# Weight halves interleaved word by word, and the merge's streams moved to 256-byte boundaries, in a float32 attention block on one core

## The chip, the core and the metric

The kernel runs on one core of a Trainium2 chip. The metric is device time in microseconds (us); lower is better. Three runs of the kernel before took 586.53 to 587.0 us, median 586.82. The profile below is of one further execution; its instructions span 584.6 us.

## What is computed

One hybrid decoder block on 512 tokens plus 16 learned meta tokens, model width 1,024, in float32. Cut to what matters here:

```python
u = rmsnorm(h, pre_norm_g[l])
proj = u @ w_in[l]
(cq, ckv, k_pe_raw, z_mla, fq, fk, fv, f_logit, z_fox, gate_a, gate_b) = jnp.split(proj, split_idx, axis=-1)
q = (rmsnorm(cq, ...) @ w_uq[l])            # 16 heads, 64 + 32 columns
kv = (rmsnorm(ckv, ...) @ w_ukv[l])
o_mla = causal_block_attention(q_m, k_m, v_mla, MLA_SCALE)
y_mla = (o_mla * jax.nn.silu(z_mla)) @ w_br_mla[l]
o_fox = causal_block_attention(fox_heads(fq), fox_heads(fk), fox_heads(fv), FOX_SCALE, cum)
y_fox = (o_fox * jax.nn.silu(z_fox)) @ w_br_fox[l]
mixed = (jax.nn.sigmoid(gate_a) * y_mla + jax.nn.sigmoid(gate_b) * y_fox) @ w_out[l]
h = h + rmsnorm(mixed, post_norm_g[l])
```

`proj` has 7,600 columns; 1,024 rows of weights stand behind each. Nearly all the work is products with weights.

## The kernel before, in words

**Precision by halves.** A float32 operand is split into an upper half (the value rounded to the engine's `float32r`) and a lower half (the rest). A product `w x a` becomes three matmuls into the same accumulator: upper weight with upper activation, upper weight with lower activation, lower weight with upper activation. `unit` (the work of one output tile) and `passes` issue them in that order for each of the eight 128-row blocks `k`.

**Who is stationary.** In a matmul `mm(out, x, y)` the operand `x` (128 x 128) is loaded into the array and `y` streams past it. For all projections (`fq`, `fk`, `v`, `z`, `pg`, `mq`, `mk`, `ppe`) and for the branch outputs (`py` and the merge's products `x`, `y`, `z`) the weight halves are stationary and the activations stream: 512 real tokens at once, or two streams of 272 and 256 tokens where the meta tokens are needed. In the last stage, the product with `w_out`, it is the other way: activations are stationary and 512 columns of weights stream.

**Where the operands lie.** `uTh` and `uTl` (the normed input, transposed, both halves) have rows of 576 words per block, so that the 512 real tokens of every block start at a multiple of 256 bytes. A weight passes through the pool `wp` with three buffers each of `wraw` (as it comes from memory), `wh` and `wl` (its halves), 128 x 1,024 words each; all start at a multiple of 256 bytes. In the built program `gh` and `gl` (halves of the gated attention output) start at 90,880 and 107,264 bytes, both 0 modulo 256; `a1h`, `a1l`, `a2h`, `a2l` (sums of it) at 161,216, 165,312, 169,408 and 177,600, and `tb0` to `tb3` (columns of `w_out`) from 128,448, all 192 modulo 256.

**How a weight is split.** `wload` issues the DMA into `wraw` on SP's queue. `wsplit` then has ScalarE (ACT) cast `raw` to `wh`, and POOL (later VectorE, DVE) compute `raw - wh` into `wl` in `split_lo`. `q_mla` does the same for two gathered pieces; `take` in `pair_py` splits sums of weights in halves of a room. Loads run up to three units ahead, splits about one to two units ahead.

**Order.** TensorE's order is written by hand (a list of steps for each attention stage: scores, then filling units, then values). The order on ACT and DVE comes from a scheduler that follows priorities and when operands and rooms become free. There are 16 attention stages of about 20 us; then the merge: four pairs of output tiles by products of 256 columns (seven products of 12 matmuls each per pair, three with streams from `a1`/`a2`, four from `gh`/`gl`), alternating with gate units `pg`; then `py`; then the product with `w_out`.

Every matmul and every weight load stands at line 98 of the profile (the helper `mm`), every subtraction at line 104, the casts at 131, 607 and 1119.

Of the kernel before, what the change touches and what calls it, by code (L numbers as in the profile page):

```python
# [11 lines left out]
F32 = mybir.dt.float32  # L12
F32R = mybir.dt.float32r
# [42 lines left out]
def block_kernel(ctx: ExitStack, tc: tile.TileContext, x, meta_tokens, pre_norm_g, w_in, fox_forget_b,  # L56
# [6 lines left out]
    wout = w_out[0].rearrange("(k p) f -> p k f", p=128)  # L63
# [20 lines left out]
    wp = ctx.enter_context(tc.tile_pool(name="wp", bufs=3))  # L84
    uid = [0]
# [3 lines left out]
    def dma(out, src, start=None):  # L89

        with tc.issue_after(sums_out[0]) if written[0] and sums_out else nullcontext():
            ins = (start or nc.sync.dma_start)(out=out, in_=src)
        if written[0]:
            tc.keep_in_program_order(ins)
        return ins.ins

    def mm(*a, **k):
        nc.tensor.matmul(*a, **k)  # L98
# [4 lines left out]
    def split_lo(eng, lo, src, hi):  # L103
        return eng.tensor_tensor(out=lo, in0=src, in1=f32(hi), op=ALU.subtract)  # L104

    def wload(srcs):

        uid[0] += 1
        u = uid[0]
        raw = wp.tile([128, 1024], F32, tag="wraw", name=f"wraw{u}")  # L110
        n = 0
        parts = []
        for src in srcs:
            dims = src.shape[1:]
            w = int(np.prod(dims))
            names = "abcd"[: len(dims)]
            pat = f"p ({' '.join(names)}) -> p {' '.join(names)}"
            rv = raw[:, n : n + w].rearrange(pat, **{c: d for c, d in zip(names, dims)})
            dma(rv, src)
            parts.append((n, w))  # L120
            n += w
        return u, raw, parts, n

    low = [nc.gpsimd]

    def wsplit(ld):

        u, raw, parts, n = ld
        wh, wl = (wp.tile([128, 1024], F32R, tag=t, name=f"{t}{u}") for t in ("wh", "wl"))
        with tc.issue_after(behind[0]) if behind else nullcontext():  # L130
            nc.scalar.copy(wh[:, :n], raw[:, :n])  # L131
        with tc.issue_after(held[0]) if held else nullcontext():
            split_lo(low[0], wl[:, :n], raw[:, :n], wh[:, :n])
        return [(wh[:, o : o + w], wl[:, o : o + w]) for o, w in parts]

    def wunit(srcs):
        return wsplit(wload(srcs))

    def weights(srcs, wrap):

# [12 lines left out]
    def by_k(part, nk):  # L153

        h, l = (t.rearrange("p (k f) -> p k f", k=nk) for t in part)
        return (lambda k: h[:, k, :]), (lambda k: l[:, k, :])
# [390 lines left out]
    with ExitStack() as att:  # L547
# [41 lines left out]
        def load_qp(pr):  # L589
            dma(f32(QP), qpe_dram[2 * pr : 2 * pr + 2].rearrange("h i x f s -> (h i x f) s"))  # L590

        def q_mla(pr):
            ld = []

            def load():
                if not ld:
                    ld.append(wload([wuq[:, :, 192 * pr : 192 * pr + 192], wukv[:, 256 * pr : 256 * pr + 256]]))

            def get():
                load()  # L600
                u, raw, _, _ = ld[0]
                wh, wl = (wp.tile([128, 1024], F32R, tag=t, name=f"{t}{u}") for t in ("wh", "wl"))
                cuts = [(raw[:, 0:384].rearrange("p (b e) -> p b e", e=96)[:, :, 0:NOPE], lambda t: t[:, 0:256].rearrange("p (b e) -> p b e", e=NOPE)),
                        (raw[:, 384:640].rearrange("p (h a e) -> p a h e", h=2, a=2), lambda t: t[:, 256:512].rearrange("p (a h e) -> p a h e", a=2, h=2))]
                for src, to in cuts:
                    with tc.issue_after(behind[0]) if behind else nullcontext():
                        nc.scalar.copy(to(wh), src)
                for src, to in cuts:
                    split_lo(nc.gpsimd, to(wl), src, to(wh))
                w = mw[pr] = [(wh[:, o : o + 128], wl[:, o : o + 128]) for o in range(0, 512, 128)]  # L610
                return (lambda k: w[k][0]), (lambda k: w[k][1])
            get.load = load

            halves = hl_done(("q", 0, pr), S, S)

            def q_done(i, ps):
                halves(i, ps)
                if pr:
                    load_qp(pr)
            return unit(f"mq{pr}", get, cq_act, 2, REAL, q_done)  # L620
# [441 lines left out]
    with ExitStack() as mg:  # L1062
        mg.enter_context(tc.manual_schedule(engines={mybir.EngineType.PE}))
        m1 = mg.enter_context(tc.tile_pool(name="m1", bufs=1, side="right"))
# [6 lines left out]
        tb = [m1.tile([128, HK, 512], F32, tag=f"tb{n}", name=f"tb{n}") for n in range(4)]  # L1071
        a1 = [m1.tile([128, HK, 256], F32R, tag=n, name=n) for n in ("a1h", "a1l")]
        a2 = [m1.tile([128, HK, S], F32R, tag=n, name=n) for n in ("a2h", "a2l")]
        mx = gT[0]
        sh, sl = ([t.rearrange("p k s -> p (k s)")[:, 1024 * j : 1024 * j + 1024].rearrange("p (k s) -> p k s", k=HK)
                   for j in range(4)] for t in uT0)
# [41 lines left out]
        def split_to(to, src):  # L1118
            nc.scalar.copy(to[0], src)  # L1119
            split_lo(nc.vector, to[1], src, to[0])  # L1120
# [6 lines left out]
        def comb(out, p, q, op=ALU.subtract):  # L1127
            nc.vector.tensor_tensor(out=out, in0=p, in1=q, op=op)  # L1128

        def pair_py(i, br):  # L1130

            j, g, wb = i + HK, gT[br], wbr[br]
            ra, rb = (wload([wb[:, :, 128 * f : 128 * f + 128]])[1] for f in (i, j))
            yield
            b11, b21, b12, b22 = ra[:, 0:512], ra[:, 512:], rb[:, 0:512], rb[:, 512:]
            X, Y, Z = (sp.tile([128, 512], F32, tag="s", name=f"{n}{i}{br}")[:, 0:256] for n in "xyz")
            c11, c21, c12, c22 = g[:, i, lo_], g[:, i, up], g[:, j, lo_], g[:, j, up]
            th1, th2 = ths[i, br], ths[j, br]
            room = []

            def take(src):
                if not room:
                    uid[0] += 1
                    hl = [wp.tile([128, 1024], F32R, tag=t, name=f"{t}{uid[0]}") for t in ("wh", "wl")]
                    room.extend([[t[:, sl] for t in hl] for sl in (slice(0, 512), slice(512, 1024))])
                to = room.pop(0)
                split_to(to, src)
                return to

            def prod(ps, a, w, first, last):  # L1150
                q = 0
                for k in range(HK):
                    for wx, ax in ((w[0], a[0]), (w[0], a[1]), (w[1], a[0])):
                        mm(ps, wx[:, 128 * k : 128 * k + 128], ax[:, k], start=(first and q == 0), stop=(last and q == 11),
                           skip_group_check=True)
                        q += 1

            def gated(dst, th, ts, ps, add):
                if add:
                    held[:] = [nc.vector.tensor_tensor(out=dst, in0=ps, in1=dst, op=ALU.add).ins]  # L1160
                return nc.vector.scalar_tensor_tensor(out=dst, in0=th[:, ts], scalar=1.0, in1=dst if add else ps, op0=ALU.add, op1=ALU.mult)

            w11 = take(b11)
            comb(b11, b12, b11)
            t1 = take(b11)
            yield
            comb(b12, b22, b12)
            comb(b11, b22, b11)
            t2 = take(b11)
            prod(X, A11, w11, True, False)  # L1170
            nc.scalar.copy(c11, X)
            w21 = take(b21)
            prod(Z, S1, t1, True, False)
            nc.scalar.copy(c22, Z)
            t3 = take(b12)
            comb(b21, b21, b11)
            prod(X, S2, t2, False, False)
            nc.scalar.copy(c12, X)
            w22 = take(b22)
            prod(Y, A12, w21, True, True)  # L1180
            gated(c11, th1, lo_, Y, True)
            t4 = take(b21)
            prod(X, S3, t3, False, False)
            gated(c22, th2, up, X, True)
            read = held[0]
            prod(Z, S4, w22, False, True)
            gated(c12, th2, lo_, Z, True)
            held[:] = [read]
            prod(X, A22, t4, False, True)
            closed[i] = gated(c21, th1, up, X, False).ins  # L1190
# [21 lines left out]
        for i in range(HK):  # L1212
# [5 lines left out]
            if i == 0:  # L1218
                for n, (q, c) in enumerate(((0, 0), (0, 1), (1, 1), (1, 0))):
                    for half in range(2):  # L1220
                        k0 = HK * q + 2 * half
# [30 lines left out]

        def plain(kb, n, c):
            k0 = HK * kb + 2 * c
            return by_k(wunit([wout[:, k0 : k0 + 2, 512 * n : 512 * n + 512]])[0], 2)

        def summed(n, c):
            uid[0] += 1
            raw = tb[n][:, 2 * c : 2 * c + 2].rearrange("p k f -> p (k f)")
            return by_k(wsplit((uid[0], raw, [(0, 1024)], 1024))[0], 2)  # L1260

        def put_in(n, c, to):
            raw = tb[n][:, 2 * c : 2 * c + 2]
# [130 lines left out]
```

## Time and profile before

| | |
|---|---|
| three timed runs | 586.53, 586.82, 587.0 us |
| profiled execution, span of its instructions | 584.6 us |
| granted TensorE clock, mean | 0.997 of full speed |
| 46 to 374 us (attention): TensorE busy | 328.00 of 328 us |
| 374 to 415 us: TensorE busy | 41.00 of 41 us |
| 415 to 540 us (merge): TensorE busy | 125.00 of 125 us |
| bytes read from HBM | 62.36 MB |

How to read it: the profiled execution's own time is not listed apart from its span; what lies around the span is seen by its distance to the timed runs, about 2.2 us. Matmuls overlap, so the duration of one (some 390 ns for 512 columns) is longer than the distance from one start to the next; in the chain of waits, given in order of time, a row has the start, the length and the count of a run of matmuls, and length by count is that distance. The chain names a run by the tile it writes. PEld is the weight load, which is laid under the matmul before it.

### The profile page before, as it was taken

The page shows a single profiled execution, that of the slowest core. Times are in us where ns is not written, and L with a number is a line of the kernel's source. Part 1 is how long each engine was busy: PE and PEld are TensorE (multiplying, and loading weights), DVE is VectorE, ACT ScalarE, POOL GpSimd, SP SyncE. Part 2 cuts the span into 40 slices and gives each one's busy share as a digit, 9 for nine tenths or more (in the row PEclk, how much of TensorE's full clock was granted, in tenths as well). Part 3 has the DMA queues.
Part 4 walks back from the last instruction along what each step waited for, and adds up shares of the span by engine and source line. Part 5 has one row for each costly group of instructions (what it writes and reads, how often), then busy time and mean ns, then how long its engine had stood idle before and what let it go on. Part 6 is the DMA issues. An engine that isn't in the chain of part 4 may idle for free.

```text
span 584.6 us, 11115 instructions
## 1 busy us (share of the span) xinstructions
PE 575.7 (98%) x3841; PEld 496.8 (85%) x3841; DVE 416.4 (71%) x1156; ACT 357.4 (61%) x816; POOL 199.4 (34%) x270
## 2 busy tenths in 40 slices
PE   8999999999999999999999999999999999999996
PEld 6989889889889888888898898878998998888884
DVE  5854877885776775767758748896647876468966
ACT  7856774893774775767748747944343462443762
POOL 4317745464468462654554634510000000000000
PEclk9999999999999999999999999999999999999998
DMA  8535599989977999988986976977722534233503
GB/s 295 122 83 163 127 176 230 231 195 248 177 167 158 228 191 206 219 172 207 183 176 180 219 154 147 183 172 236 233 73 72 145 104 144 78 109 108 217 0 144
DMA packets 220000, 97.47 MB, mean 167 GB/s; under 512 B 131456, under 2 KB 209672, under 8 KB 219944
## 3 DMA queue, kind: packets, MB, share of 16 engines
q1 hardware_dynamic: 219944, 96.77, 70.3%
q8 instruction: 30, 0.49, 0.3%
q14 instruction: 26, 0.21, 0.1%
HBM read 62.36 MB, written 3.97 MB: 113 GB/s over the span
## 4 chain that ended last, share of the span: by engine, by line
PE 96%; ACT 1%; DMA 1%; issue 0%; SPq 0%; DVE 0%; POOL 0%; DVEq 0%; ACTq 0%; POOLq 0%
PE z L98 19%; PE pg L98 15%; PE v L98 9%; PE fk L98 8%; PE st L98 8%; PE fq L98 8%; PE x L98 8%; PE py L98 7%; PE ov L98 5%; PE psm L98 3%; PE y L98 2%; PE mq L98 2%; PE mk L98 1%; PE ppe L98 1%; DMA wsr<-in_w_in_dram 1%; ACT uTh L371 0%
## 5 line engine op out<-in xcount | busy, mean ns | idle before, releaser
L104 POOL TENSOR_TENSOR wl<-wraw,wh 128x1024 fp32r<-128x1024 f32 (+2 forms) x61 | 118.3, 1947 | 112.2 <-ACT wh L131 80.5
L131 ACT CAST wh<-wraw 128x1024 fp32r<-128x1024 f32 (+1 forms) x72 | 74.6, 1042 | 56.4 <-PE py L98 16.8
L826 ACT ACTIVATE sf<-sf,nb 128x272 f32<-128x272 f32 (+3 forms) x128 | 72.7, 569 | 11.5 <-DVE nb L791 10.6
L865 DVE SCALAR_TENSOR_TENSOR pn<-sf,ri,pn 128x512 f16<-128x512 f32 (+3 forms) x128 | 69.6, 609 | 1.6 <-ACT pn L861 1.5
L104 DVE TENSOR_TENSOR wl<-wraw,wh 128x512 fp32r<-128x512 f32 (+1 forms) x55 | 52.2, 950 | 23.9 <-ACT wh L1119 17.8
L861 ACT ACTIVATE pn<-sf,ri 128x128 f16<-128x128 f32 (+3 forms) x128 | 59.7, 548 | 0.5 <-DVE ri L831 0.5
L98 PE MATMUL z<-uTh,wh 128*128 128x512 f32 x128 | 50.9, 398 | 0.0
L98 PE MATMUL pg<-uTh,wh 128*128 128x512 f32 x128 | 50.2, 392 | 0.0
L98 PE MATMUL z<-uTl,wh 128*128 128x512 f32 x128 | 50.1, 391 | 0.0
L98 PE MATMUL z<-uTh,wl 128*128 128x512 f32 x128 | 50.0, 390 | 0.0
L98 PE MATMUL pg<-uTl,wh 128*128 128x512 f32 x128 | 49.9, 390 | 0.0
L98 PE MATMUL pg<-uTh,wl 128*128 128x512 f32 x128 | 49.8, 389 | 0.0
L706 DVE TENSOR_REDUCE vsc<-v 128x1 f32<-128x272 f32 (+1 forms) x32 | 13.2, 433 | 39.8 <-PE v L98 39.8
L98 PE MATMUL st<-hlk,hlq 64*128 64x272 f32 (+4 forms) x480 | 41.3, 299 | 0.0
L1119 ACT CAST wh<-wraw 128x512 fp32r<-128x512 f32 x28 | 17.3, 618 | 37.9 <-DVE wraw L1128 17.0
L98 PE MATMUL v<-uTh,wl 128*128 128x256 f32 (+1 forms) x128 | 36.5, 285 | 0.0
L98 PE MATMUL fk<-uTl,wh 128*128 128x256 f32 (+1 forms) x128 | 36.4, 285 | 0.0
L98 PEld LDWEIGHTS st<-hlk,hlq 64*128 64x128 f32 x480 | 33.0, 186 | 4.1 <-ACT vh L725 2.8
L98 PE MATMUL fk<-uTh,wh 128*128 128x256 f32 (+1 forms) x128 | 36.4, 285 | 0.0
L98 PE MATMUL v<-uTl,wh 128*128 128x256 f32 (+1 forms) x128 | 36.4, 285 | 0.0
L98 PE MATMUL fk<-uTh,wl 128*128 128x256 f32 (+1 forms) x128 | 36.4, 285 | 0.0
L98 PE MATMUL v<-uTh,wh 128*128 128x256 f32 (+1 forms) x128 | 36.4, 284 | 0.0
(295 smaller groups left out, 1612.3 us busy)
## 6 DMA issues: line engine op xcount, KB each, us to landing
wraw<-in_w_in_dram SPq DMA_DIRECT2D x56, 512.0 KB, 4.8
cbp<-c_dram SPq DMA_DIRECT2D x16, 264.0 KB, 4.1
wraw<-in_w_br_fox_dram SPq DMA_DIRECT2D x8, 512.0 KB, 4.5
tb<-in_w_out_dram SPq DMA_DIRECT2D x8, 512.0 KB, 5.4
wraw<-in_w_br_mla_dram SPq DMA_DIRECT2D x8, 512.0 KB, 4.3
wraw<-in_w_out_dram SPq DMA_DIRECT2D x6, 512.0 KB, 3.6
xr<-in_x_dram SPq DMA_DIRECT2D x4, 512.0 KB
out_dram<-yo SPq DMA_DIRECT2D x8, 256.0 KB, 2.0
```

The source lines that it names most:

```text
L98: nc.tensor.matmul(*a, **k)
L104: return eng.tensor_tensor(out=lo, in0=src, in1=f32(hi), op=ALU.subtract)
L131: nc.scalar.copy(wh[:, :n], raw[:, :n])
L706: nc.vector.tensor_reduce(out=sc[:, i : i + 1], in_=ps, op=ALU.max, axis=AX.X, apply_absolute_value=True)
L826: exps[b // 3] = nc.scalar.activation(sf, sf, AF.Exp, bias=sums["nb"][:, h, b : b + 1], scale=-1.0, accum_out=sums["su"][:, h, b : b + 1]).ins
L861: normed[:] = [nc.scalar.activation(hi, sf, AF.Copy, scale=rib).ins]
L865: nc.vector.scalar_tensor_tensor(out=lo, in0=sf, scalar=rib, in1=hi, op0=ALU.mult, op1=ALU.subtract)
L1119: nc.scalar.copy(to[0], src)
```

## The change

The halves of one weight lie in one room of 2,048 words. With `mixed`, word 0 is the first upper half, word 1 the first lower half, and so on: each half is read and written with a step of two words (8 bytes). The rooms for the product with `w_out`, where weights stream, stay unmixed: the upper half in the first 1,024 words, the lower in the second. A tile of 48 words that nothing uses is added to the pool `m1`; in the built program it moves `a1`, `a2` and `tb` down by 192 bytes, to 161,024 and so on, 0 modulo 256. The rooms start at 66,304, 74,496 and 82,688 bytes, the same space as before.

```diff
+    def halves_of(u, mixed=True):
+        w = wp.tile([128, 2048], F32R, tag="w", name=f"w{u}")
+        w = w.rearrange("p (n l) -> p n l", l=2) if mixed else w.rearrange("p (l n) -> p n l", l=2)
+        return w[:, :, 0], w[:, :, 1]
+
-    def wsplit(ld):
+    def wsplit(ld, mixed=True):
 
         u, raw, parts, n = ld
-        wh, wl = (wp.tile([128, 1024], F32R, tag=t, name=f"{t}{u}") for t in ("wh", "wl"))
+        wh, wl = halves_of(u, mixed)
...
@@ q_mla
-                wh, wl = (wp.tile([128, 1024], F32R, tag=t, name=f"{t}{u}") for t in ("wh", "wl"))
+                wh, wl = halves_of(u)
...
+        m1.tile([128, 48], F32, tag="shift", name="shift4")
...
@@ take, in pair_py
-                    hl = [wp.tile([128, 1024], F32R, tag=t, name=f"{t}{uid[0]}") for t in ("wh", "wl")]
+                    hl = halves_of(uid[0])
...
@@ plain and summed, the product with w_out
-            return by_k(wunit([wout[:, k0 : k0 + 2, 512 * n : 512 * n + 512]])[0], 2)
+            return by_k(wunit([wout[:, k0 : k0 + 2, 512 * n : 512 * n + 512]], False)[0], 2)
```

The order of instructions on TensorE, POOL and SP is the same as before. On ACT it moves in one way, once per attention stage and alike in the merge. Before, ACT in the third stage (`sil` is the gate of a finished `z` unit, `wh` the upper half of the weights of a unit one stage on, `hlq` and `hlk` the split queries and keys):

```order
L861 ACTIVATE pn_716<-sf_1445,ri_1443 128x4x128
L131 CAST wh_1799<-wraw_1539 128x1024 [waits DMAHW7_49,PE_49,Pool_49]
L741 ACTIVATE sil_1588<-z_1541 128x512 [waits PE_49]
L247 CAST hlq_1606<-mq_1599 128x512 [waits PE_49]
L247 CAST hlk_1642<-mk_1638 128x272 [waits PE_49]
```

The same place after the change:

```order
L866 ACTIVATE pn_714<-sf_1434,ri_1432 128x4x128
L746 ACTIVATE sil_1576<-z_1529 128x512 [waits PE_49]
L136 CAST w_1785<-wraw_1527 128x1024 [waits DMAHW7_49,Pool_49]
L252 CAST hlq_1593<-mq_1586 128x512 [waits PE_49]
L252 CAST hlk_1628<-mk_1624 128x272 [waits PE_49]
```

The cast into the room has gone behind `sil`. On TensorE at the start of a `z` unit, before (uTh and uTl stream, wh and wl are stationary):

```order
L98 MATMUL z_1541<-uTh,wh_1535 128x512
L98 MATMUL z_1541<-uTl,wh_1535 128x512
L98 MATMUL z_1541<-uTh,wl_1536 128x512 [waits Pool_49]
L98 MATMUL z_1541<-uTh,wh_1535 128x512
L98 MATMUL z_1541<-uTl,wh_1535 128x512
```

After:

```order
L98 MATMUL z_1529<-uTh,w_1524 128x512
L98 MATMUL z_1529<-uTl,w_1524 128x512
L98 MATMUL z_1529<-uTh,w_1524 128x512 [waits Pool_49]
L98 MATMUL z_1529<-uTh,w_1524 128x512
L98 MATMUL z_1529<-uTl,w_1524 128x512
```

Nothing moved there: the third matmul still is the one that waits for the lower half, though both halves now lie in one tile.

More of the change, by code (lines that the diff above doesn't have):

```diff
@@ L134, in wsplit, with wunit @@
         return [(wh[:, o : o + w], wl[:, o : o + w]) for o, w in parts]
-    def wunit(srcs):
-        return wsplit(wload(srcs))
+    def wunit(srcs, mixed=True):
+        return wsplit(wload(srcs), mixed)
     def weights(srcs, wrap):
@@ L1259, in summed @@
             raw = tb[n][:, 2 * c : 2 * c + 2].rearrange("p k f -> p (k f)")
-            return by_k(wsplit((uid[0], raw, [(0, 1024)], 1024))[0], 2)
+            return by_k(wsplit((uid[0], raw, [(0, 1024)], 1024), False)[0], 2)
         def put_in(n, c, to):
```

## The prediction

> **What bounds the kernel now.** I read the page's shares of busy time first, then its chain of waits, then that chain in order of time, where the length of a run of matmuls divided by their count gives the time from one matmul's start to the next. (A matmul's own duration in the groups, some 390 ns, overlaps its neighbours and says little.)
>
> ```profile
> span 584.6 us, 11115 instructions
> PE 575.7 (98%) x3841; PEld 496.8 (85%) x3841; DVE 416.4 (71%) x1156; ACT 357.4 (61%) x816; POOL 199.4 (34%) x270
> PE 96%; ACT 1%; DMA 1%; issue 0%; SPq 0%; DVE 0%; POOL 0%; DVEq 0%; ACTq 0%; POOLq 0%
> ```
>
> The chain that ends last is 96% TensorE. A change counts here by what it does to the spacing of matmuls, or by making TensorE wait. The spacing, from the chain in order of time (start, length, what):
>
> ```profile
> 83.46 5.67 PE fq L98 x24
> 89.13 2.96 PE fk L98 x24
> 97.92 2.88 PE fk L98 x24
> 104.95 5.66 PE z L98 x24
> 418.44 10.91 PE pg L98 x48
> 502.44 38.08 PE py L98 x168
> 408.61 1.43 PE x L98 x12
> 411.48 1.38 PE x L98 x12
> 415.66 1.36 PE z L98 x12
> ```
>
> - `py`, 512 columns streamed per matmul: 38.08/168 = 226.7 ns each; `pg` 10.91/48 = 227.3.
> - `fk`, its first 24 with 272 columns: 123.3 ns; its second 24 with 256: 120.0 ns.
> - The merge's 256-column products: 119.2 with the stream from gh/gl (first x row), 115.0 from a1 (second), 113.3 from a2 (z).
>
> Between 256 and 512 columns lie 226.7 - 120.0 = 106.7 ns, so a column costs 0.417 ns, and 512, 272 and 256 columns cost 213.3, 113.3 and 106.7. What is left is a part that does not grow with the stream: 13.4 ns (`py`), 14.0 (`pg`), 10.0 (`fk` 272), 13.3 (`fk` 256), 12.5 (gh), 8.3 (a1), 6.7 (a2). Every matmul of this kernel has one weight load of its own (both counts 3841), laid under the matmul before it. The fixed part is the same under 256 and 512 columns, so it goes with the load or the handover, not with the stream's length; and it differs between streams of one width. In the built program gh, gl, uTh, uTl (real tokens) and all weight rooms start at 0 modulo 256 bytes, a1 and a2 at 192: the same load costs 12.5 to 13.4 ns under a stream that starts in step with the room, 6.7 to 8.3 under one 64 bytes off. I read this as load and stream getting in each other's way at some relative positions. `fq` and `z` have more (236.3 and 235.8 ns), but part of that lies where each run starts, and I leave it as it is.
>
> **The change part by part.**
>
> *Interleaved halves.* A weight load of 128 columns now reads every second word over 1,024 bytes, instead of 512 bytes in a row. A load and a stream of 256 columns together take 113.3 ns at best, so while the stream walks its first 1,024 bytes the old load walked about 512: the stream overtook it by about two 256-byte periods per load. With step 2 both walk at about one pace and keep the distance they started with. If the disturbance comes from overtaking, most of it goes; if it comes from standing at the same place, it comes all the time. No strided weight load is in this trace, so the price has to be bounded. Counts, one row of the three products of each kind:
>
> ```profile
> L98 PE MATMUL z<-uTh,wh 128*128 128x512 f32 x128 | 50.9, 398 | 0.0
> L98 PE MATMUL pg<-uTh,wh 128*128 128x512 f32 x128 | 50.2, 392 | 0.0
> L98 PE MATMUL fq<-uTh,wh 128*128 128x512 f32 x64 | 25.9, 405 | 0.0
> L98 PE MATMUL py<-gh,wh 128*128 128x512 f32 x64 | 24.9, 389 | 0.0
> L98 PE MATMUL v<-uTh,wl 128*128 128x256 f32 (+1 forms) x128 | 36.5, 285 | 0.0
> L98 PE MATMUL fk<-uTh,wh 128*128 128x256 f32 (+1 forms) x128 | 36.4, 285 | 0.0
> ```
>
> Three times these: 1,152 matmuls of 512 columns; 768 of `fk` and `v`, half with 256 and half with 272. The merge adds 192 of 256 columns on gh/gl and 144 on a1/a2 (four pairs of 84 matmuls; three of seven products use a1/a2). The latent streams add 168 by the loops of the code: mq, mk and the other branch's v 48 each over eight pairs, ppe 24.
>
> Lower end: the fixed part vanishes, 1,152 x 13.4 + 384 x 13.3 + 384 x 10.0 + 192 x 12.5 + 144 x 7.5 + 168 x 13 = 30.0 us off. Upper end: the largest fixed part that the trace has, on a latent stream, by starts of single matmuls:
>
> ```profile
> 110.69 0.40 PE L98 MATMUL mq<-cTl,wh 128*128 128x512 f32 x1
> 110.93 0.39 PE L98 MATMUL mq<-cTh,wl 128*128 128x512 f32 x1
> ```
>
> 0.24 us, so 27 ns, twice the ordinary 13.4; on everything that is about 31 us more. I take the value of the nearest row with little disturbance, a2's 6.7 ns, since a stream that no longer overtakes the load should do no worse than one that is overtaking it at a good distance. The gain by groups: 1,152 x 6.7 = 7.7 us; `fk`/`v` at 256, 384 x 6.7 = 2.6; at 272, 384 x 3.3 = 1.3; gh/gl, 192 x 6 = 1.2; a1/a2 about 0.1; latents 168 x 6.7 = 1.1. Sum 14.0 us.
>
> [...]
>
> *a1, a2 and tb moved by 192 bytes.* With contiguous rooms this would cost 144 x (13.3 - 7.5) = 0.8 us; with interleaved ones it is in the sum above. In the last stage a1 and a2 are the stationary side and the weights (not interleaved there) stream as before: 0 to 0.3 us either way.
>
> *Writing and reading with step 2 off TensorE.* The high-half cast writes with step 2; the low-half subtraction reads one operand and writes with step 2. Today:
>
> ```profile
> L104 POOL TENSOR_TENSOR wl<-wraw,wh 128x1024 fp32r<-128x1024 f32 (+2 forms) x61 | 118.3, 1947 | 112.2 <-ACT wh L131 80.5
> L131 ACT CAST wh<-wraw 128x1024 fp32r<-128x1024 f32 (+1 forms) x72 | 74.6, 1042 | 56.4 <-PE py L98 16.8
> 89.18 2.71 POOL L104 TENSOR_TENSOR wl<-wraw,wh 128x1024 fp32r<-128x1024 f32 x1
> 92.18 0.29 PE L98 MATMUL v<-uTh,wl 128*128 128x272 f32 x1
> ```
>
> What hides them is that splits run ahead of use. The tightest place is the last pair of rows: the subtraction ends at 91.89 and its first reader starts at 92.18, 0.3 us later. In the merge:
>
> ```profile
> 416.10 1.22 DVE L104 TENSOR_TENSOR wl<-wraw,wh 128x1024 fp32r<-128x1024 f32 x1
> 418.44 6.60 PE pg L98 x29
> ```
>
> The split ends at 417.32, its unit starts at 418.44 and reads the low half two matmuls (0.45 us) later: 1.6 us spare, four times over. Bounds: nothing, if an element costs the same; doubled, about 2.1 us at 89.18, 1.5 at two other early splits together, and (1.05 + 1.22 - 1.6) = 0.7 at each of four merge places: 6.4 us. I take 0: the cast's 1,042 ns for mostly 1,024 columns is about one element per ns, a pace per element rather than per stretch of memory, and that row is the nearest there is.
>
> *Order.* On ACT one cast per stage stands behind the gate activation or the next cast, about 1 us later, since its room now comes free with the last read of either half. In stage 3 of the trace:
>
> ```profile
> 112.31 1.04 ACT L131 CAST wh<-wraw 128x1024 fp32r<-128x1024 f32 x1
> 124.50 5.67 PE fq L98 x24
> ```
>
> The cast ends at 113.35 and its unit starts at 124.50: 11 us of cover, so I count nothing for 1 us. Waits of the third matmul of a unit on the low half stay as they are; PE's order is unchanged.
>
> Total: the span of 584.6 us becomes 570.6. The timed median is 586.82, 2.2 us above the span; those 2.2 us (start and end) stay: 572.8 us. Own range of this case: half the gain (580) to a fixed part of about 2 ns (561).
>
> **The rivals.**
>
> A. *Nothing changes for the stream.* [...] For it: 13.3 to 13.4 ns, nearly one number, in `fk` 256 and `py`. Against it: 6.7 ns under a2. The time: only the a1/a2 move counts, +0.8 us: 587.6. Chance 0.13.
>
> B. *Slower: the load disturbs the stream twice as often.* If each stretch of memory that a load touches costs the stream something, 1,024 bytes cost twice what 512 do: 26.7 ns, which `mq` shows to be possible. +13.4 x 1,152 + 13.3 x 384 + 10 x 384 + 12.5 x 192 + 19 x 144 + 13 x 168 = 31.7 us: 618.5. It decides as soon as the mean fixed part rises above today's 13: in step and at the same position, load and stream could also collide without end. Against it: a stream moved by only 64 bytes halves the cost, which a price per byte loaded would not show. [...] Chance 0.19.
>
> C. *Slower: the splits become late.* Step 2 doubles the split's cost and TensorE's pace stays: 6.4 us as above, 593.2; the place is 85 to 92 us and the four merge pairs. It decides from about 0.3 us more per subtraction. [...] Chance 0.07.
>
> **How the numbers follow.** Forecast (faster by about 14 us) 0.61, A 0.13, B 0.19, C 0.07. The likeliest time is 572.8 us. The range runs from 560 to 600: it holds the forecast nearly whole, A and C, and leaves out B's full price (0.19 less its mild end) and the last stretch of gain. The forecast's own range is 561 to 580. A measurement of this kernel can tell about 0.2% (1.2 us) from no change: faster 0.61, same 0.13 (A at +0.8 us lies within it), slower 0.26 (B and C).
>
> **What would show it.** Right: `py` in the chain at about 220 ns per matmul (now 226.7), `fk` 256 at 113 (now 120.0), the merge's gh and a2 products alike near 113, and DVE, ACT and POOL no later for TensorE. A: `py` at 226.7 and the a2 products up from 113.3 to 120. B: `py` towards 240, `fk` 256 towards 133. C: `py` unchanged, gaps on TensorE near 90 us and at the merge's gate units, longer L104 rows. The prediction is wrong if the streams' spacing does not fall, or if it falls but TensorE gains waits of more than a few us.

## The result, and the profile after

The changed kernel takes 597.17 us (median of four runs, 597.04 to 597.8), the kernel before 586.89 beside it. The ratio is 1.0176, with a 95% interval of 1.0162 to 1.0191: 10.3 us slower, where 14 us faster had been forecast. That lies inside the stated range of 560 to 600 us, which had been drawn wide for the rivals, but outside the forecast's own range of 561 to 580. From the page of the changed kernel, its span, its busy times and its chain of waits:

```profile
span 595.6 us, 11106 instructions
PE 585.8 (98%) x3841; PEld 508.2 (85%) x3841; DVE 415.1 (70%) x1156; ACT 363.3 (61%) x816; POOL 202.0 (34%) x270
PE 90%; POOL 3%; DMA 2%; ACT 2%; issue 1%; DVE 1%; SPq 1%; DVEq 0%; POOLq 0%; ACTq 0%
```

TensorE's busy time grew by 10.1 us (575.7 before), nearly as much as the span (11.0, from 584.6): TensorE waits little longer, its matmuls stand further apart. The busy time of the weight load, PEld, grew by 11.4 us over 3,841 loads. The chain is 90% TensorE where it was 96%, mainly because ahead of 72.55 us it now runs over the other engines, to the late split shown further down. Rows of it with start, length and count that answer to those of before:

```profile
84.91 5.79 PE fq L98 x24
90.70 3.06 PE fk L98 x24
112.90 1.39 PE mq L98 x6
142.10 2.88 PE fk L98 x24
425.30 11.31 PE pg L98 x48
436.60 1.44 PE x L98 x12
439.48 1.44 PE x L98 x12
422.42 1.44 PE z L98 x12
512.07 39.57 PE py L98 x168
578.87 10.89 PE x L98 x48
```

Length by count, before and after:

| stream | before | after |
|---|---|---|
| `py`, 512 columns | 226.7 ns | 235.5 |
| `pg`, 512 | 227.3 | 235.6 |
| `fq`, 512 | 236.3 | 241.3 |
| `mq` (latent stream), 512 | 233.3 | 231.7 |
| `fk`, 272 | 123.3 | 127.5 |
| `fk`, 256 | 120.0 | 120.0 |
| merge, gh (first `x` row), 256 | 119.2 | 120.0 |
| merge, a1 (second `x` row) | 115.0 | 120.0 |
| merge, a2 (`z` row) | 113.3 | 120.0 |

(The row of `mq` before has 1.40 us for 6, at 110.62.) Every stream of 512 columns from uTh, uTl, gh or gl is 5 to 9 ns slower; the latent stream of `mq`, which was slow before, is not. 272 columns lose 4 ns, 256 columns nothing except where a1 and a2 stood well before. The product with `w_out` (last row) has unmixed rooms: 226.9 ns. The work off TensorE, by groups:

```profile
L104 POOL TENSOR_TENSOR w<-wraw,w 128x1024 fp32r<-128x1024 f32 (+2 forms) x61 | 120.9, 1990 | 119.3 <-ACT w L136 88.6
L136 ACT CAST w<-wraw 128x1024 fp32r<-128x1024 f32 (+1 forms) x72 | 80.3, 1120 | 53.6 <-PE py L98 18.5
```

The cast with step 2 takes 7% more (1,120 against 1,042 ns), POOL's subtraction 2% (1,990 against 1,947). For the cast it is the step that costs this: in the run without interleaving, further down, the two casts between 69 and 80 us take 1,034 and 1,064 ns, and the six from `tb` in the changed kernel, whose rooms are unmixed, have a median of 1,050 where the 72 of the row have 1,134. There is one place where a late split is waited for, in the first full stage:

```profile
68.46 1.45 ACT sf L831 x4
...
71.35 1.16 DVE w L104
72.55 1.90 PE z L98 x7
```

VectorE's subtraction for a `z` unit (the row at 71.35) ends at 72.51 and the matmul that reads it starts at 72.55. In the kernel before the same subtraction began 4.3 us earlier, by its row in time:

```profile
67.04 1.22 DVE L104 TENSOR_TENSOR wl<-wraw,wh 128x1024 fp32r<-128x1024 f32 x1
```

The wait itself is short: the timeline has the matmul before at 71.86, so 0.69 us pass where 0.23 is usual, some 0.5 us lost. Twice more TensorE waits in this execution that it did not before, ahead of the values `ov` at 105.07 (for the transposing DMA into `pt`) and at 125.26, 0.31 and 0.40 us of idle time by the timeline, together 0.7 us. The profile of the same kernel without its tile of 48 words (`mixed_noshift`, below) has neither, so they are not taken for a cost of the change.

### The profile page after: what moved, and what is told of

It reads as the page before. It is cut to its first block, busy times and chain, and to the rows that moved or that the text cites. A ratio compares the mean times of both kernels' runs of the same rounds, so it can differ in the third digit from the quotient of the medians.

```text
span 595.6 us, 11106 instructions
## 1 busy us (share of the span) xinstructions
PE 585.8 (98%) x3841; PEld 508.2 (85%) x3841; DVE 415.1 (70%) x1156; ACT 363.3 (61%) x816; POOL 202.0 (34%) x270
## 4 chain that ended last, share of the span: by engine, by line
PE 90%; POOL 3%; DMA 2%; ACT 2%; issue 1%; DVE 1%; SPq 1%; DVEq 0%; POOLq 0%; ACTq 0%
PE z L98 18%; PE pg L98 14%; PE v L98 8%; PE fq L98 8%; PE py L98 8%; PE x L98 8%; PE fk L98 7%; PE st L98 7%; PE ov L98 5%; PE psm L98 2%; PE y L98 2%; PE mq L98 2%; POOL w L104 1%; PE mk L98 1%; DMA wsr<-in_w_in_dram 1%
## 5 line engine op out<-in xcount | busy, mean ns | idle before, releaser
L104 POOL TENSOR_TENSOR w<-wraw,w 128x1024 fp32r<-128x1024 f32 (+2 forms) x61 | 120.9, 1990 | 119.3 <-ACT w L136 88.6
L136 ACT CAST w<-wraw 128x1024 fp32r<-128x1024 f32 (+1 forms) x72 | 80.3, 1120 | 53.6 <-PE py L98 18.5
L98 PE MATMUL z<-uTh,w 128*128 128x512 f32 x256 | 86.2, 397 | 0.3 <-DVE w L104 0.3
L98 PE MATMUL pg<-uTh,w 128*128 128x512 f32 x256 | 82.6, 398 | 0.0
L104 DVE TENSOR_TENSOR w<-wraw,w 128x512 fp32r<-128x512 f32 (+1 forms) x55 | 52.1, 958 | 31.3 <-ACT w L1125 22.4
L98 PEld LDWEIGHTS pg<-uTh,w 128*128 128x128 f32 x256 | 50.0, 195 | 10.4 <-issue 0.3
L98 PEld LDWEIGHTS z<-uTh,w 128*128 128x128 f32 x256 | 49.5, 194 | 10.3 <-DVE w L104 0.7
L98 PE MATMUL pg<-uTl,w 128*128 128x512 f32 x128 | 50.6, 395 | 0.0
L98 PE MATMUL z<-uTl,w 128*128 128x512 f32 x128 | 50.4, 394 | 0.0
L98 PE MATMUL fk<-uTh,w 128*128 128x272 f32 (+1 forms) x256 | 50.0, 287 | 0.0
```

## The experiments

Two theories stood against each other at the start of the experiments. **Theory S (spacing):** a strided load slows the matmuls themselves, and long streams pay. **Rival:** the time is lost elsewhere, to the shared rooms and their order, the late splits, or the moved a1 and a2.

### A table of matmul rows

A kernel that leaves the block out, returns `x` and issues only rows of 48 matmuls, in the order of the real units (two streams, two halves), with one thing changed from row to row:

```python
"one": [room[:, 1024 * l : 1024 * l + 1024].rearrange("p (k n) -> p k n", k=8) for l in range(2)],
"two": [room[:, 0:2048].rearrange("p (k n l) -> p k n l", k=8, l=2)[:, :, :, l] for l in range(2)],
"four": [room.rearrange("p (k n l) -> p k n l", k=8, l=4)[:, :, :, l] for l in range(2)],
...   # cut
for q, (w, a) in enumerate(((h, sa), (h, sb), (l, sa))):
    nc.tensor.matmul(ps[:m, :n], w[:, k], a[:, k, off : off + n], start=(r == k == q == 0),
                     stop=(r == 1 and k == 7 and q == 2))
```

> This kernel leaves the block out: it returns x and only times rows of 48 matmuls with 128 stationary columns each, other engines idle, so that the spacing of matmuls is seen by itself. Step of the weights one, two or four words; streams of 512, 384, 256 and 128 columns (w, m, h, q) that start at 0, 64, 128 or 192 bytes modulo 256 (a, b, c, d); weights with 64 columns (half). Theory 1, the load disturbs the stream by the memory that it walks: one_a_w 226.7 ns, two_a_w 233 to 236, four_a_w about 246; and since a disturbance under 256 columns is hidden by the load's own length, one_a_h and two_a_h both 120. halftwo (64 columns over the same bytes as one) costs as much as one. Theory 2, the price goes with the number of loaded columns and the rise to 233 in the whole kernel comes from other engines' strided writes: two_a_w stays at 226.7 here, halftwo costs as halfone. If a load of step two takes longer by itself, two_a_q (128 columns streamed) is longer than one_a_q. The offset: one_d_h near 113 as a2 had, one_a_h 120.

Rows of its chain, in order of time. In a name stand the step of the load, the place of the stream (a, b, c, d: moved by 0, 64, 128, 192 bytes) and its columns (w 512, m 384, h 256, q 128):

```profile
28.11 10.88 PE one_a_w L97 x48
47.34 5.75 PE one_a_h L97 x48
53.09 5.31 PE one_a_q L97 x48
58.40 11.26 PE two_a_w L97 x48
77.98 5.76 PE two_a_h L97 x48
83.74 5.59 PE two_a_q L97 x48
89.34 11.05 PE one_b_w L97 x48
100.39 5.44 PE one_b_h L97 x48
173.55 11.05 PE two_d_w L97 x48
235.00 11.09 PE four_a_h L97 x48
```

At 512 columns step 2 costs 8 ns: 226.7 to 234.6 (233.3 in the two later tables). At 384 and 256 it costs nothing (174.0 and 173.3; 119.8 and 120.0). The kernel gives no other engine work in these rows, so 7 to 8 of the 8 to 9 ns that `py` and `pg` lose in the kernel are made by load and stream alone. The second thing to see is `one_b`: a stream moved by 64 bytes is quicker at 256 columns (113.3) and slower at 512 (230.2). The place that gains at 256 columns loses at 512. The place of a2 itself, 192 bytes, did not repeat its 113.3 here: 117.7 at 256 columns, where about 113 was expected, and 233.3 at 512. A load of half the columns (`halfone`) does not help at 512 either (11.04 us for 48, 230.0), though it does at 256 (5.45 us, 113.5); with step 2 it takes 231.7 at 512. At 128 columns, whose own time would be 53 ns, the load sets the pace: 110.6 ns at step 1, 116.5 at step 2. At step 4 it sets it at 256 columns too, 231.0 ns, and 128 columns took 233.1 there; the mean duration of a load (PEld) is 329 ns in these rows, against 192 at step 1 and 196 at step 2. The granted clock had a mean of 0.981 over this run.

### The change without interleaving

```diff
-    def halves_of(u, mixed=True):
+    def halves_of(u, mixed=False):
-    def wsplit(ld, mixed=True):
+    def wsplit(ld, mixed=False):
-    def wunit(srcs, mixed=True):
+    def wunit(srcs, mixed=False):
```

> The change without its interleaving: one room of 2048 words per weight, upper half first and lower half behind it everywhere, a1 and a2 at 0 modulo 256. Theory 1 (the step costs on TensorE): py back at 226.7 ns, fk with 272 columns at 123.3, time 587.5 to 588.0, the rest over before being a1/a2's 0.8 us and some 0.3 us from the later cast. Rival (the shared room and the cast moved behind the gate activation cost the time): stays above 590.

588.93 us (588.54 to 590.06), ratio 1.0036 (1.0023 to 1.0048). Rows of its chain:

```profile
70.92 1.16 DVE w L104
72.12 1.89 PE z L98 x7
84.42 5.67 PE fq L98 x24
419.63 10.91 PE pg L98 x48
504.36 38.08 PE py L98 x168
```

These spacings are those of before, and only the merge's products differ (a1 and a2 have 1.44 us for 12, 120.0), so the interleaving carries about 8.5 of the 10.3 us. What remains is seen from the starts: `fq` stands at 84.42 instead of 83.46, 0.96 us late; `pg` at 419.63 instead of 418.44, 1.19 late; `py` at 504.36 instead of 502.44, 1.92 late. The first is the `z` unit that waits for a late split, here too, with contiguous halves: it comes with the shared rooms, not with step 2. The rest grows through the merge, where a1 and a2 stand.

### Only a1, a2 and tb moved

```diff
         a2 = [m1.tile([128, HK, S], F32R, tag=n, name=n) for n in ("a2h", "a2l")]
+        m1.tile([128, 48], F32, tag="shift", name="shift4")
```

> The kernel before with a1, a2 and tb moved to 0 modulo 256 and nothing else. If the start of a stream relative to the room sets the fixed part, the merge's products from a1 and a2 go from 115.0 and 113.3 to 119 to 120 ns and the time rises by 0.8 us to 587.7. If a1 and a2 were faster for another reason, they stay at 113 to 115 and the time stays at 586.9.

587.61 us (587.33 to 588.35), ratio 1.0010 (1.0001 to 1.0020); the span is 585.4, 0.8 more than before. The merge's products on a1 and a2, by the chain:

```profile
411.47 1.44 PE x L98 x12
415.79 1.44 PE z L98 x12
```

120.0 ns each, from 115.0 and 113.3: 144 matmuls by 5 to 7 ns are 0.7 to 1.0 us, as forecast. (The medians give 0.4; the interval of the ratio reaches from 0.1 to 1.2 us.)

### The kernel before, with its main streams 192 bytes off

```diff
-ROW = 64
+ROW = 48
-    uT0 = [const.tile([128, KD, ROW + L - META], F32R, tag=n, name=n) for n in ("uTh", "uTl")]
+    uT0 = [const.tile([128, KD, 64 + L - META], F32R, tag=n, name=n) for n in ("uTh", "uTl")]
```

> The kernel before with the normed input's real tokens starting at 192 modulo 256 instead of 0. If a start 64 bytes off halves the fixed part at any width, fk and v with 256 columns go from 120 to 113 and fq, z and pg from 227 to about 220: some 10 us less, 577. If the offset helps only where the load is as long as the stream (256 columns), only fk and v's 256-column halves gain, 384 x 6.7 = 2.6 us, and the 272-column ones (now at 128) and the 512-column ones may lose as the latent streams do (231 to 240 ns): 584 to 592.

590.78 us (590.49 to 592.46), ratio 1.0068 (1.0053 to 1.0083): slower by 3.6 us. If a2's low fixed part came from its position alone, streams of every width should have gained. The 256 columns do, the 512 lose:

```profile
83.83 5.79 PE fq L98 x24
140.13 2.72 PE fk L98 x24
506.72 38.10 PE py L98 x168
```

`fk` with 256 columns takes 113.3 ns instead of 120.0, as a2 did; `fq` takes 241.3 instead of 236.3; `py`, whose streams gh and gl were not moved, stays at 226.8. Nothing is strided here, and the spacing of `fq` is that of the changed kernel. This decides against the prediction's step within the kernel itself: one move of one pair of streams takes 6.7 ns off the short ones and puts 5 ns on the long ones.

### From which length on

The same kind of table, with more widths, and with the room moved instead of the stream (`rone`, `rtwo`: 64 bytes further on):

```python
r2 = room2[:, 16:2064]
views["rone"] = [r2[:, 1024 * l : 1024 * l + 1024].rearrange("p (k n) -> p k n", k=8) for l in range(2)]
views["rtwo"] = [r2.rearrange("p (k n l) -> p k n l", k=8, l=2)[:, :, :, l] for l in range(2)]
```

> Leaves the block out and returns x; it only times rows of 48 matmuls with the other engines idle, so its time is no time of the block. A name has the kind of weights (one: halves in a row, two: every second word, rone and rtwo the same 64 bytes further on, twohh and twoll only the upper or only the lower half, same: one block again and again), the words by which the stream is moved, and its columns. In the first table of such rows step 2 cost 8 ns a matmul at 512 columns (226.7 to 234.6) and nothing at 256 and 384. Theory 1, the cost belongs to long streams: step 2 costs nothing up to about 416 columns, and it sets in between 416 and 512 and grows there. Theory 2, the cost belongs to 512 columns alone (a full 2,048 bytes): 496, 480 and 448 are alike for both steps. Theory 3, load and stream meet by relative position: rone at a stream moved by 16 words is 226.7 again as without both moves, and rone at 0 is like the stream moved the other way, 233; by absolute position rone at 0 stays 226.7. If two loads of alternating parity were the trouble, twohh would be 226.7; I expect 234. The kernel's own 272 columns moved by 48 words: 123.3 with one, 127.5 with two.

Rows of the chain; the first has 512 columns, the next four 448 and 416, and the last two are `rone` with the stream at 0 and moved by 16 words (the count of 49 has one matmul of the row behind it):

```profile
38.56 11.20 PE two L103 x48
92.09 9.90 PE one L103 x48
102.00 9.77 PE two L103 x48
111.76 8.96 PE one L103 x48
120.72 8.96 PE two L103 x48
207.82 11.43 PE rone L103 x49
219.01 10.90 PE rone L103 x48
```

Neither of the first two theories is quite right. At 320 and 416 columns (146.7 and 186.7) both steps have 13.3 ns above the columns' time of 0.417 ns each; 288 columns have 11.7 at step 1 and 13.3 at step 2, and 272 moved by 48 words take 123.6 and 127.7, as in the kernel. Above 416, the extra goes up at some widths for either step: 19.6 ns for step 1 at 448 (206.3; step 2 has 16.9, 203.5), 13.3 again at 512. Step 2 is at 20 there (233.3). So 512 columns in step with a contiguous room are a good case among long streams, and step 2 loses it. The third theory held: with room and stream both moved, the row is 227.1 again; with the room alone moved, 233.3, which is what the first table had for a stream moved the other way (`one_d`, 233.3). What counts in these four rows is the place of one relative to the other. Loads of one parity only gave 233.3 too, so the change between upper and lower half is not what costs.

### Interleaving only for short streams

```diff
-        return unit(f"fk{pr}", win_w(O_FK, pr), u_act, KD, ALLT, hl_done(("k", 1, pr), L, HALF), keybank[0])
+        return unit(f"fk{pr}", win_w(O_FK, pr, True), u_act, KD, ALLT, hl_done(("k", 1, pr), L, HALF), keybank[0])
...
-                get, nk, act = win_w(O_FV, pr), KD, u_act
+                get, nk, act = win_w(O_FV, pr, True), KD, u_act
...
-                    hl = halves_of(uid[0])
+                    hl = halves_of(uid[0], True)
```

with `mixed=False` everywhere else.

> The changed kernel with interleaved rooms only for fk, v and the merge's products, whose streams have 256 and 272 columns; the units with 512 columns have their halves in a row. Theory 1 (only 512 columns pay for step 2, 272 a little): 588.9 of the same change without any interleaving, plus 384 x 4 ns at 272 columns = 1.5 us, so 590.5, and py at 226.7 ns. Rival (every strided load costs some 8 ns in the kernel, where other engines run, whatever the width): 588.9 + 768 x 8 ns + 336 x 8 ns = 597.7.

590.8 us (590.11 to 591.41), ratio 1.0054 (1.0036 to 1.0073), against 590.5 expected and 597.7 by the rival.

```profile
90.78 3.04 PE fk L98 x24
506.41 38.08 PE py L98 x168
```

`fq` (5.67 us for 24) and `py` are back at 236.3 and 226.7, `fk` at 272 columns takes 126.7. The 512-column units are thus worth 597.17 - 590.8 = 6.4 us of the loss (7.2 by the profiles' spans, 595.6 and 588.4).

### The changed kernel with its main streams moved

The diff of the fourth experiment, made in the changed kernel.

> The changed kernel with the real tokens of uTh and uTl at 192 instead of 0 modulo 256 bytes. In the table of matmul rows, step 2 at 512 columns cost 234.6 ns in step with the room and 230.1 with the stream at 192. If position matters in the kernel as there: pg, z and fq (1,088 matmuls) at some 4.5 ns less, about 592. Rival, the position is of no account once the load is strided: 597. With halves in a row the same move made the kernel slower by 3.6 us; if it does that here too, 600.

593.6 us (593.5 to 594.5), ratio 1.0106 (1.0088 to 1.0124): 3.6 us better than the change, where the same move costs the kernel before 3.6 us.

```profile
443.81 11.04 PE pg L98 x48
502.68 5.60 PE pg L98 x24
508.27 39.19 PE py L98 x168
```

`fq` falls to 239.2 (5.74 us for 24; 241.3 in the change), and `pg` takes 11.04 us for 48 in the merge, 230.0. That is the table's row `two_d_w`, 230.2. In the first table, with the stream moved by 0, 64, 128 and 192 bytes, 512 columns take 226.7, 230.2, 232.3 and 233.3 ns under a contiguous load and 234.6, 233.3, 231.7 and 230.2 under a strided one: what is good for the one is bad for the other, but the best strided place of the four (230.2) remains worse than the best contiguous one (226.7).

Two more things are in these rows. The last `pg` unit, whose streams and rooms stand at the same places modulo 256 bytes as the other, takes 233.3 ns and not 230.0; it runs between two runs of `py`, the other behind products of 256 columns. And `py`, whose streams were not moved, takes 233.3 instead of the 235.5 (39.57 us for 168) that it has in the change, and also in the next run, which was on the same chip as this one. So load, stream and their places do not settle the pace alone.

### The change without the tile of 48 words

```diff
-        m1.tile([128, 48], F32, tag="shift", name="shift4")
```

> The changed kernel without the tile of 48 words, so a1, a2 and tb at 192 modulo 256 bytes as before. Without interleaving the tile cost 0.6 to 0.8 us. In the table of rows step 2 took 120.0 ns at 256 columns at every position, so with interleaved rooms it should be worth nothing: 597.2, a1 and a2 at 120.0. Rival, the favourable position survives interleaving: 113 to 115 ns on 144 matmuls, 596.4.

598.21 us (597.82 to 598.41), ratio 1.0179 (1.0158 to 1.0199). The second `x` row of a pair, with its stream from a1:

```profile
439.77 1.44 PE x L98 x12
```

It has 120.0 ns, and the merge's other products 119 to 120. Once the loads are strided, a1 and a2 gain nothing from their old place; the rival's 113 to 115 ns is excluded. Against its own runs of the kernel before, the median lies 0.9 us above the change; these rows do not explain that.

### Is a place better than the kernel before to be had?

If 256 columns ran at 113.3 ns wherever the stream is 64 bytes off, rooms of their own place for `fk`, `v` and the merge would be worth up to 384 x 6.7 + 192 x 6 ns = 3.7 us. Two more tables looked at that, with contiguous rows of 272 and 256 columns first, then with the room's start moved by 256 to 8,192 bytes:

```python
def halves(kind, b):
    r = room[:, b : b + 2048]
    ...   # cut: the views, as above, of r
```

> Leaves the block out and returns x; it only times rows of 48 matmuls with halves in a row and the other engines idle, so its time is no time of the block. A name says by how many words the stream is moved from the room's place modulo 256 bytes, and its columns. Theory 1, only the distance of stream and room modulo 256 bytes counts: 512 columns moved by 64 words are 226.7 ns again, as by 0, and by 1, 2 and 60 words 227 to 233. Rival, the distance counts in full: by 64 words differs from by 0. At 256 columns the earlier rows stand: 120.0, 113.3, 120.0 and 117.7 by 0, 16, 32 and 48 words, and 12 and 20 words lie between their neighbours. What 272 columns take by 0, 16 and 32 words is open (123.6 by 48): between 120.0 if all is as good as 256 columns by 16 words, and 126.7 if as bad as by 0.

> Leaves the block out and returns x; it only times rows of 48 matmuls with the other engines idle, so its time is no time of the block. The room starts 0, 256, 512, 1,024, 2,048, 4,096 or 8,192 bytes further on (at, in words), the stream is moved by 0, 16 or 48 words. Theory 1, the place modulo 256 bytes settles it: step 2 at 512 columns is 233 to 235 ns from every start, step 1 is 226.7, and 256 columns moved by 16 words are alike from all starts (113.3 as in the first table, or 118 as in the third). Theory 2, the distance counts beyond 256 bytes: 256 columns by 16 words go to and fro between 113 and 118 as the start moves by 256 bytes, and step 2 at 512 columns varies too, perhaps down to 227, where only the place of the rooms would have been unlucky. The first and the last row are the same and tell how well a row repeats: within 0.1 us of 48 matmuls, 2 ns each.

The first of them, by rows of its chain (the number in front of w says by how many words the stream is moved):

```profile
58.23 5.66 PE one_by16w_256c L103 x48
69.59 5.47 PE one_by48w_256c L103 x48
85.95 10.88 PE one_by64w_512c L103 x48
96.83 11.36 PE one_by1w_512c L103 x48
```

512 columns moved by a whole 256 bytes are 226.7 again, moved by one word 236.7. But 256 columns by 16 words took 117.9 here, and by 48 words 114.0: the other way round than in the first table (113.3 and 117.7). The second, where the first row is repeated as the last, and rows of one kind from all starts run together:

```profile
28.11 5.66 PE one_at_by16w_256c L93 x48
33.77 78.40 PE two_at_by0w_512c L93 x336
112.17 54.40 PE one_at_by0w_512c L93 x240
234.41 5.66 PE one_at_by16w_256c L93 x48
```

Over all seven starts (0 to 8,192 bytes further on) step 2 takes 233.3 ns in the mean (78.40 over 336), and over the five up to 4,096 bytes step 1 takes 226.7 (54.40 over 240), the figures of a single row, so these places of the rooms would not have saved the change. The repeated row agrees, 117.9 both times, with rooms and streams at the very addresses of the first table, where it was 113.3. In that table the row stood behind one of 512 columns at the same place; here it stands behind others. The tables also ran on different chips, so they do not show by themselves which of the two it is; that `pg` and `py` had two paces on one chip, above, speaks for what ran before. The same operands can thus run at two paces. Moving rooms by it would be a gamble on 113 to 118, with 272 columns at 125.2 in step (6.01 us for 48) against 123.3 now; no version faster than the kernel before came out of this.

## Why the prediction was wrong

**The step that failed** is "I take the value of the nearest row with little disturbance, a2's 6.7 ns". Two thoughts carried it. One was that "the fixed part is the same under 256 and 512 columns, so it goes with the load or the handover, not with the stream's length". It was the same (13.3 and 13.4) only at the one place where both streams stood: in the table, moved by 64 bytes, 256 columns fall to 6.7 above their columns' time and 512 rise to 16.9, and in the kernel, moved by 192 bytes, `fk` fell by 6.7 ns and `fq` rose by 5. The other was the picture of a stream that overtakes the load. By it the load that keeps pace should be disturbed less; the streams lose more than before, or the same, depending on the width: `py` has 22.2 ns above its columns' time where 6.7 had been taken (235.5 - 213.3), `fk` with 256 columns keeps its 13.3. The prediction's own trace could have been read more carefully: a2 is a row of 256 columns, and most of the gain, 7.7 of 14.0 us, was booked on streams of 512, for which no row with a low fixed part existed.

By terms, in differences of medians, each against the runs of the kernel before on its own chip (586.89, 587.01 or 587.21):

| term | forecast | measured, and from what |
|---|---|---|
| 512 columns, latents with them | -8.8 | +6.5: change less the one with short streams only (10.28 - 3.79) |
| `fk`, `v`, merge | -5.2 | +2.1: the latter less the change without interleaving (3.79 - 1.72) |
| shared rooms and order | 0 | +1.3 (1.72 - 0.40); one wait of 0.5 to 1.0 us is seen in the profiles |
| a1, a2 and tb moved | 0.8 with contiguous rooms | +0.4; 0.8 by the span |
| sum | -14.0 | +10.3 |

**Bound.** Right: TensorE's spacing set the time, and most of the change lies in it.

**Off TensorE.** The price per element was nearly right: 0 taken, 7% on ACT and 2% on POOL measured, and the merge's splits are on time. The order was not: a cast "about 1 us later" and "11 us of cover" were read from stage 3 and taken for all. In the first full stage the cast of one `z` unit has gone behind the exponentials, not only behind the gate activation, and starts at 69.8 us instead of 64.2; the subtraction begins at 71.3 instead of 67.0, and TensorE waits some 0.5 us. Without interleaving it waits there too: the subtraction ends at 72.08, the matmul starts at 72.12, and the next `fq` unit is 0.96 us later than before.

**a1 and a2.** The +0.8 us with contiguous rooms was right. That the term vanishes in the sum was not, since 256 columns stay at 120.0 under step 2.

**The rivals.** A failed in its one number, `py` at 226.7. C failed: there is one late split and not a row of them. B had the sign and `py` near its 240 (235.5), but its price per byte loaded would have charged 256 columns too, which stayed at 120.0 where it said 133; so it came out at 31.7 us instead of 8.6 (6.5 + 2.1). The tables show that load and stream bear on each other: moving the room alone by 64 bytes makes 233.3 of 226.7 ns, and moving the stream along with it brings 227.1 back. Nor does the load's own time grow evenly with the bytes that it walks: where it sets the pace, step 2 costs 5% (116.5 against 110.6 ns) and step 4 about twice the time (231.0).

**What stays open** is why. The tables show a pace that depends on the load's step (226.7 to 233.3 or 234.6 ns at 512 columns), on the distance of load and stream within 256 bytes (226.7 by 0 and by 64 words, 236.7 by one word) and on the stream's length (step 2 costs nothing at 256 and 416 columns). Which part of the chip does it, why step 2 is free at 416 columns (186.7 both) and not at 512, and why the same row can run at two paces, is not.

## What to carry to other kernels

A spacing read off one stream is a fact about that width and that place, and perhaps about what ran before it (`pg` took 230.0 and 233.3 ns in one execution): price a stride or a move on the width that has most of the matmuls, and measure a row of them alone before a kernel's loads are changed. A load with step 2 was hidden here under 256 columns as well as one with step 1 (120.0 and 119.8 ns), and still slowed the 512 columns that hid it (226.7 to 234.6). Two buffers made into one come free together, which lost some 0.5 us in the first full stage here, so look for the stage with the least cover, not a typical one.

## What the runs showed of the hardware that was not expected

- In step 1, 512 columns take 226.7 ns with room and stream at the same place modulo 256 bytes, 236.7 with the stream one word off, 233.3 at 60 words and 230.2 at 16 words off.
- The time above 0.417 ns per column is not constant: 13.3 ns at 416 and 512 columns, 19.6 at 448.
- The same move of the streams, by 192 bytes, made `fk` with 256 columns faster (120.0 to 113.3 ns) and `fq` with 512 slower (236.3 to 241.3).
- The same 256-column row took 113.3 ns in one table and 117.9 in another, on another chip, and `py` took 233.3 and 235.5 in two kernels on one chip.
- A load of 64 columns instead of 128 makes a 512-column row slower, 230.0 against 226.7, and a 256-column row faster, 113.5 against 119.8.
